# Loading half of one chunk by sixteen small transfers in a DMA-bound softmax

## The chip, the cores and the metric

The kernel runs on one core of a Trainium2 chip. The metric is device time in microseconds of one execution. The sixteen DMA engines move a transfer in packets, one row of a chunk each (32,000 packets of 32 KB for 250 full transfers of 128 rows in the kernel before). Each engine reports on the transfer's semaphore when its share is done; this moment is a **landing**, and each transfer of the kernel before has sixteen.

## The reference

```python
batch, seq, vocab = 16, 256, 32768
logits: float32 [16, 256, 32768], temperature = 1.0
scaled = logits / temperature
scaled = scaled - scaled.max(axis=-1, keepdims=True)
exp_scaled = np.exp(scaled)
return exp_scaled / exp_scaled.sum(axis=-1, keepdims=True)
```

That is a softmax over 4096 rows: 537 MB are read and 537 MB are written.

## The kernel before

Each row is cut into two halves, so there are 8192 half rows of 16384 numbers. 128 half rows, one per SBUF partition, make a group; a group is two chunks of [128 x 8192] float32, 4 MB each. There are 64 groups and 128 chunks. A chunk lives in one of six slots: it is loaded, reduced to its maximum on VectorE, exponentiated in place on ScalarE, scaled in place by both, and stored from the same slot. All transfers are issued by SyncE.

```python
_CW = 8192; _BUFS = 6; _LAST_DMA = 4096

def load(i):
    g, c = divmod(i, C)
    xs = xpool.tile([P, CW], fp32, tag="x", name="xs")
    slots[i] = xs
    # the first and the last group are loaded in halves of 4096 columns
    for s, n in spans(CW, _LAST_DMA if g in (0, G - 1) else CW):
        nc.sync.dma_start(out=xs[:, s : s + n],
                          in_=x[g * P : (g + 1) * P, c * CW + s : c * CW + s + n])
...
# order: loads of chunks 0 to 5, store 0, then store i and load i + 5
order = [("L", i) for i in range(min(_BUFS, n_chunks))] + [("S", 0)]
for i in range(1, n_chunks):
    order.append(("S", i))
    if i + _BUFS - 1 < n_chunks:
        order.append(("L", i + _BUFS - 1))
```

(Wrappers that keep the program order are left out above.)

## Time and profile before

The time before is 2494.8 us (median of 4, 2492.84 to 2495.53).

| what | value |
|---|---|
| DMA engines, share of slices at 90% or more | all but the last |
| rate over the span, over 1000 to 2000 us | 431 GB/s, 433 GB/s |
| packets of 32 KB (one row of a chunk): usual time | 1.213 us |
| packets of 16 KB: usual time | 0.611 us |
| landings of the last transfer, first and last of 16 engines | 2482.4 and 2492.9 us |

The page of the kernel before, busy shares and the first rows of its 40 time slices (a digit 9 is 90% or more):

```profile
span 2493.8 us, 2234 instructions
DVE 1487.4 (60%) x964; ACT 1405.0 (56%) x455; POOL 0.2 (0%) x4
...
DMA  9999999999999999999999999999999999999998
GB/s 412 433 430 432 429 431 432 433 433 434 433 434 432 435 432 435 432 435 431 436 431 435 432 434 433 434 433 433 433 433 433 433 433 434 434 433 434 432 431 368
```

VectorE and ScalarE have 40% to spare; the DMA engines have nothing. All slices but the first and the last lie at 429 to 436 GB/s. So the whole game is played for the last half per cent, the 431 GB/s over the span against the 433 GB/s from 1000 to 2000 us.

In this text the **shortfall** of a stretch is its length minus the bytes moved in it divided by 433.3 GB/s (sixteen packets of 32 KB every 1.21 us), with each packet's bytes spread evenly over its time; it is worked out from the packet records. Before, it is 3.6 us up to 80 us (mostly the start) and 2.0 us from 80 to 460 us. **Stretching** is the sum, over all packets, of the time above 1.213 or 0.611 us, where it exceeds 0.05 us. Nearly all of it falls before 460 us, in bursts 19.4 us apart, where the engines go over from a load to a store all at once: up to 230 us each burst starts in the last 1 to 3 us before a load lands (from 108 us on for the load that lands at 110.2 us). The worst burst comes earlier, from 58 us on, before the load that lands at 61.7 us; from 60 to 61 us the rate is 285 GB/s.

What SyncE waits for before it issues a transfer, in the kernel before (total, times, longest):

```profile
SPq L64 <- DMA out_dram<-xs: 2246.9, 122, 19.6
SPq L75 <- DVE xs L160: 73.4, 4, 39.7
SPq L224 <- DMA out_dram<-xs: 30.7, 3, 21.1
```

L64 is the load, L75 the store. Loads wait for the store that frees their slot; no load waits for another load.

The beginning of the chain of waits of the kernel before, from 8 us on (start, length, what):

```profile
2.68 29.61 DMA xs<-in_logits_dram
...
48.26 7.21 ACT xs L163 x2
...
55.48 26.44 DMA out_dram<-xs
...
82.38 38.48 DMA out_dram<-xs
...
121.31 38.66 DMA out_dram<-xs
```

The stores 0 and 1 are issued at 51.9 and 55.5 us, when they are computed, while the queues still hold loads up to about 62 us. From 82 us on the chain runs store by store in steps of about 39 us, four transfers each.

### The profile page before, as it was taken

To read this page: it belongs to the slowest core of one execution; us is meant where nothing else is said; L and a number is where in the kernel's file an instruction comes from. 1 tells how busy PE (TensorE), PEld (TensorE's weight loads), DVE (VectorE), ACT (ScalarE), POOL (GpSimd) and SP (SyncE) were. 2 spreads that over 40 slices of the span, in tenths; PEclk is the share of its full clock that TensorE was granted. 3 is DMA by queue.
4 is the path that set the end of the run, shared out by engine and by line. 5 is a ranking of instruction groups with operands and counts; after the bars stand their busy time and mean duration, and the time that the engine had idled before them with its cause. 6 is when DMAs were issued, how large, how long until landed. Compare 5 with 4: busy or idle time off the path is not lost.

```text
span 2493.8 us, 2234 instructions
## 1 busy us (share of the span) xinstructions
DVE 1487.4 (60%) x964; ACT 1405.0 (56%) x455; POOL 0.2 (0%) x4
## 2 busy tenths in 40 slices
DVE  7655565556655566555665566655666566655663
ACT  5665554655556555565555655555546555465553
POOL 0000000000000000000000000000000000000000
DMA  9999999999999999999999999999999999999998
GB/s 412 433 430 432 429 431 432 433 433 434 433 434 432 435 432 435 432 435 431 436 431 435 432 434 433 434 433 433 433 433 433 433 433 434 434 433 434 432 431 368
DMA packets 37745, 1073.90 MB, mean 431 GB/s; under 512 B 4192, under 2 KB 4192, under 8 KB 4192
## 3 DMA queue, kind: packets, MB, share of 16 engines
q1 hardware_dynamic: 37728, 1073.76, 99.9%
q14 instruction: 17, 0.14, 0.0%
HBM read 536.87 MB, written 536.87 MB: 431 GB/s over the span
## 4 chain that ended last, share of the span: by engine, by line
DMA 96%; SPq 1%; ACT 1%; DVE 1%; issue 1%; ACTq 0%
DMA out_dram<-xs 93%; DMA xs<-in_logits_dram 2%; SPq L64 1%; DVE nm L107 1%; ACT xs L163 1%; ACT xs L114 0%; ACTq L224 0%; SPq L75 0%; DVE f L150 0%; ACT ee L131 0%; DVE rS L149 0%; DVE Sh L87 0%; DVE ttj L138 0%; DVE Sh L84 0%; DVE Sh L138 0%
## 5 line engine op out<-in xcount | busy, mean ns | idle before, releaser
L114 ACT ACTIVATE xs<-xs,nm 128x8192 f32<-128x8192 f32 (+1 forms) x130 | 912.1, 7016 | 972.4 <-DVE nm L107 972.4
L107 DVE TENSOR_REDUCE nm<-xs 128x1 f32<-128x8192 f32 (+1 forms) x130 | 1111.6, 8551 | 527.3 <-DMA xs<-in_logits_dram 527.3
L163 ACT ACTIVATE xs<-xs,f 128x4096 f32<-128x4096 f32 (+1 forms) x130 | 468.1, 3648 | 71.4 <-DVE f L150 71.4
L160 DVE TENSOR_SCALAR xs<-xs,f 128x4096 f32<-128x4096 f32 (+1 forms) x130 | 295.7, 2318 | 3.7 <-DVE f L150 1.8
L138 DVE CUSTOM_DVE_ANT_0 ttj<-ee,ssum 128x2 f32<-128x2 f32 x64 | 10.3, 161 | 423.8 <-ACT ee L131 423.8
L114 ACT ACTIVATION_READ_ACCUMULATOR xs<-xs,nm 128x1 f32 x130 | 24.2, 186 | 0.0
L131 ACT ACTIVATE ee<-nm,nMh 128x2 f32<-128x2 f32 x64 | 17.9, 280 | 0.0
L150 DVE TENSOR_SCALAR f<-ee,rS 128x2 f32<-128x2 f32 x64 | 14.6, 229 | 2.2
L149 DVE RECIPROCAL rS<-Sh 128x1 f32<-128x1 f32 x64 | 10.5, 164 | 2.2
L87 DVE TENSOR_TENSOR nMh<-nMh 128x1 f32<-128x1 f32 x64 | 10.2, 160 | 2.2
L87 DVE TENSOR_TENSOR Sh<-Sh 128x1 f32<-128x1 f32 x64 | 10.2, 160 | 2.2
L129 DVE TENSOR_REDUCE nMh<-nm 128x1 f32<-128x2 f32 x64 | 9.9, 155 | 2.2
L84 DVE STREAM_SHUFFLE nMh<-nMh 128x1 f32<-128x1 f32 x64 | 9.7, 151 | 0.0
L84 DVE STREAM_SHUFFLE Sh<-Sh 128x1 f32<-128x1 f32 x64 | 9.7, 151 | 0.0
L114 ACT ACT_TABLE_LOAD x1 | 1.3, 1283 | 12.9 <-DMA xs<-in_logits_dram 12.9
L138 DVE DVE_READ_ACCUMULATOR2_ANT Sh<- 128x1 f32 x64 | 5.3, 84 | 0.0
L84 DVE LOAD_MASK_SELECT Sh<-Sh x64 | 0.9, 14 | 2.8
L84 DVE LOAD_MASK_SELECT nMh<-nMh x64 | 0.9, 14 | 2.7
L210 POOL MEMSET const-bfloat16-1.0<- 128x1 bf16 x1 | 0.1, 102 | 0.0
L210 POOL MEMSET const-uint8-127<- 128x1 uint8 x1 | 0.1, 102 | 0.0
L210 POOL MEMSET const-float32-0.0<- 128x1 f32 x1 | 0.1, 99 | 0.2 <-issue 0.2
L210 POOL MEMSET const-float32-1.0<- 128x1 f32 x1 | 0.1, 99 | 0.0
## 6 DMA issues: line engine op xcount, KB each, us to landing
out_dram<-xs SPq DMA_DIRECT2D x126, 4096.0 KB, 38.2
xs<-in_logits_dram SPq DMA_DIRECT2D x124, 4096.0 KB, 29.0
xs<-in_logits_dram SPq DMA_DIRECT2D x8, 2048.0 KB, 22.3
out_dram<-xs SPq DMA_DIRECT2D x4, 2048.0 KB, 26.7
```

Source lines behind the costliest of these rows:

```text
L64: nc.sync.dma_start(out=xs[:, s : s + n], in_=x[g * P : (g + 1) * P, c * CW + s : c * CW + s + n],)
L84: nc.vector.stream_shuffle(out=v[:, j + 1 : j + 2], in_=v[:, j : j + 1], mask=mask)
L87: nc.vector.tensor_tensor(out=v[:, j + 1 : j + 2], in0=v[:, j : j + 1], in1=v[:, j + 1 : j + 2], op=op,)
L107: nc.vector.tensor_reduce(out=nm[:, k : k + 1], in_=xs[:, s : s + n], axis=X, op=A.max, negate=True)
L114: nc.scalar.activation(out=xs[:, s : s + n], in_=xs[:, s : s + n], func=Exp, bias=nm[:, k : k + 1], scale=inv_t, accum_out=ssum[:, k : k + 1],
L129: nc.vector.tensor_reduce(out=nMh[:, 0:1], in_=nm, axis=X, op=A.min)
L131: nc.scalar.activation(out=ee, in_=nm, func=Exp, bias=nMh[:, n_rounds : n_rounds + 1], scale=-1.0,)
L138: nc.vector.tensor_tensor_reduce(out=ttj, in0=ee, in1=ssum, scale=1.0, scalar=0.0, op0=A.mult, op1=A.add, accum_out=Sh[:, 0:1],)
L149: nc.vector.reciprocal(out=rS, in_=Sh[:, n_rounds : n_rounds + 1])
L150: nc.vector.tensor_scalar_mul(out=f, in0=ee, scalar1=rS)
L160: nc.vector.tensor_scalar_mul(out=xs[:, s : s + cut], in0=xs[:, s : s + cut], scalar1=f[:, k : k + 1])
L163: nc.scalar.activation(out=xs[:, s + cut : s + n], in_=xs[:, s + cut : s + n], func=Copy, scale=f[:, k : k + 1],)
```

## The change: its intent and the diff

The sixteen DMA engines start in step: all sixteen landings of a transfer lie within 0.4 us up to 52 us. While in step they all change over from loads to stores at once. The change wants to set them apart at the start, by giving them unequal work once. The means are transfers of 15, 14, ... 1 and 8 rows of 16 KB.

```diff
+_LADDER = _BUFS - 1
...
-        for s, n in spans(CW, _LAST_DMA if g in (0, G - 1) else CW):
-            tc.keep_in_program_order(
-                nc.sync.dma_start(
-                    out=xs[:, s : s + n],
-                    in_=x[g * P : (g + 1) * P, c * CW + s : c * CW + s + n],
+        for s, n in spans(CW, _LAST_DMA if g in (0, G - 1) or i == _LADDER else CW):
+            steps = [P] if i != _LADDER or s else [*range(15, 0, -1), 8]
+            p = 0
+            for m in steps:
+                tc.keep_in_program_order(
+                    nc.sync.dma_start(
+                        out=xs[p : p + m, s : s + n],
+                        in_=x[g * P + p : g * P + p + m, c * CW + s : c * CW + s + n],
+                    )
                 )
-            )
+                p += m
+            assert p == P
```

Below, "ladder" is the series of sixteen transfers, and "second half" the ordinary transfer of the other 4096 columns of chunk 5 that follows it.

## The prediction

> **What bounds the kernel now.** The sixteen DMA engines. The page's engine rows give VectorE 60%, ScalarE 56%, DMA 90% or more in every slice and 431 GB/s. The chain of waits is 93.5% stores. The packet records leave almost nothing to gain: nearly all 32,000 packets of 32 KB take 1.213 us (half-size ones 0.611 us); packets of one engine start 1.21 us apart, plus 0.01 us per transfer for the semaphore write. 256 full transfers of 9.68 us plus the start at 1.8 us give 2482 us. [...]
>
> The span is 2493.8 us because one engine is late. Landings of the last transfer: eight engines within 0.5 us of 2482.4 us, others 3 to 7 us later, the last 10.5 us later. That spread was 0.35 us until 52 us, 4.9 at 343, 6.5 at 460, then grew about 0.7 per 310 us. Two causes: (a) until 460 us packets stretch to 1.3 to 2.4 us at the switches between loads and stores, every 19.4 us, while engines are in step, some 3 us per engine; (b) instruction fetches of 8 KB cost one engine about 0.7 us each[...].
>
> **What the change does.** Sixteen transfers of m rows of 16 KB. [...] It aims at (a), worth at most 5 us on the last engine. [...]
>
> **It will not be evenly spaced.** There are eight completion semaphores, and the timeline shows SyncE waiting, ahead of a transfer, for the transfer eight before it on the same semaphore. Before, this cost nothing. Now steps 14 to 11 wait for the half loads of chunks 0 and 1 (8 to 23 us), 10, 9, 8 for chunks 2, 3, 4 (32, 42, 52 us), later ones for earlier steps. So the second half, on all engines, is issued near 57 us and starts near 58 us. [...] The first store goes out near 57.5 us instead of 51.9 us. [...]stretching falls by perhaps half; fetches stay. Lateness of the last engine: 1.6 to 4.9 (delay) + 5 (fetches) + 0 to 4 (stretching), around 9.5 us instead of 10.5. VectorE and ScalarE have slack (chunk 5 lands at 62 us, is read at 70 us).
>
> **Predicted: 2494.0 us, range 2489.5 to 2498.0.** Chances: faster by over 2% 0.005, within 2% 0.99, slower by over 2% 0.005.
>
> **Right or wrong shows in:** the timeline at 52 to 58 us (SyncE's waits between small issues, GB/s dipping); fewer stretched packets between 60 and 460 us; the spread of the last landings; the first store landing near 76 us.
>
> **What would make it wrong:** small transfers not waiting (full stagger, perhaps 2490 us); [...]ten engines in step spreading as before on top of the delay.

The sum came to 1.6 to 4.9 us (delay) + 5 us (fetches) + 0 to 4 us (stretching), taken as around 9.5 us after 2482.4 us, against 10.5 us before. The delay was the author's estimate, from an assumed share of rows for each engine. For the fetches the trace before shows seven steps of 0.75 to 0.78 us, 5.3 us together.

## More of the kernel before

The 25 executions of the kernel before go from 2492.47 to 2501.62 us (0.4%), the four of its first round from 2492.84 to 2495.53 us; all profiled runs compared here had a granted clock (the share of full clock speed that the chip allowed) of 1.0.

Rates in five stretches of the kernel before. The columns are the stretch, its length, busy time of VectorE, ScalarE and GpSimd with numbers of instructions, clock, DMA share and GB/s:

```profile
16.00:50.00 34.00, 32.23 (x17) 23.57 (x8) 0.00 (x0) 1.00 1.02 439
50.00:80.00 30.00, 28.70 (x20) 28.36 (x10) 0.00 (x0) 1.00 1.00 421
80.00:100.00 20.00, 13.70 (x10) 13.40 (x5) 0.00 (x0) 1.00 0.98 421
100.00:460.00 360.00, 209.52 (x136) 200.67 (x64) 0.00 (x0) 1.00 1.00 431
460.00:2440.00 1980.00, 1185.48 (x767) 1122.27 (x361) 0.00 (x0) 1.00 1.00 433
```

A packet's bytes are put where it starts, so short stretches are rough. What is to be seen is that 433 GB/s is reached from 460 us on, and that between 50 and 460 us a little is missing.

## The result

The time is 2510.11 us (median of 4, 2509.46 to 2510.58) against 2494.8 us: 15.3 us longer, above the range. The ratio of the fast runs is 1.0062, with a 95% interval of 1.0045 to 1.0080. (A ratio here is the mean time of one kernel's fast runs over that of the other's of the same rounds, so not quite the ratio of the medians.) So it is slower beyond doubt, and still within 2%.

The page after, in the same lines:

```profile
span 2507.7 us, 2257 instructions
DVE 1487.6 (59%) x964; ACT 1405.1 (56%) x455; POOL 0.2 (0%) x4
...
DMA  9999999999999999999999999999999999999998
GB/s 357 374 432 432 432 433 434 433 433 433 433 434 434 433 431 434 433 434 432 432 434 433 435 432 431 434 433 435 433 431 434 433 434 433 432 433 433 434 430 378
```

Only the first two slices differ much, 357 and 374 GB/s instead of 412 and 433. Each is 62 us long. The digits of the DMA share say little here: a packet counts as busy for as long as it takes, and packets took longer (1.72 instead of 0.611 us, below). The same stretches after:

```profile
16.00:50.00 34.00, 32.22 (x17) 23.49 (x8) 0.00 (x0) 1.00 1.02 439
50.00:80.00 30.00, 19.72 (x15) 27.24 (x9) 0.00 (x0) 1.00 0.78 172
80.00:100.00 20.00, 10.78 (x13) 8.10 (x4) 0.00 (x0) 1.00 1.02 441
100.00:460.00 360.00, 210.55 (x136) 198.64 (x64) 0.00 (x0) 1.00 1.00 432
460.00:2440.00 1980.00, 1186.18 (x767) 1119.21 (x358) 0.00 (x0) 1.00 1.00 433
```

Everything happens between 50 and 80 us: 172 GB/s at a DMA share of 0.78. The shortfall of that stretch goes from 0.9 to 17.7 us (+16.7), and from 80 to 460 us it falls from 2.0 to 0.6 us (-1.4). Together that is +15.3 us. The two profiled executions differ by 13.9 us (2493.8 and 2507.7 us): another 1.4 us were won after 2440 us, where the last landings lie closer together. (That the two stretches give the difference of the medians, 15.3 us, to the digit is chance.) SyncE's waits after:

```profile
SPq L68 <- DMA out_dram<-xs: 2244.0, 122, 19.3
SPq L68 <- DMA xs<-in_logits_dram: 60.5, 17, 10.6
SPq L81 <- DVE xs L166: 33.7, 3, 24.7
```

L68 is now the load. The second line is new: loads wait for loads, 17 times. The timeline of SyncE between 40 and 80 us in the kernel after shows how long the ladder takes to issue (start, length, number of transfers merged):

```profile
42.11 25.91 SPq L68 DMA_DIRECT2D xs<-in_logits_dram  x11
68.91 2.37 SPq L81 DMA_DIRECT2D out_dram<-xs  x2
```

The first line ends with the issue of the second half at 67.7 us; the first store goes out at 68.9 us instead of 51.9. The instruction records of SyncE have each transfer with the semaphore it waits for and the one it raises (the time in us):

```
 4.18  15 rows  raises 108          53.00   8 rows  waits 107, raises 107
 8.00  14 rows  waits  99, raises  99    54.70   7 rows  waits 108, raises 108
12.88  13 rows  waits 100, raises 100    56.67   6 rows  waits  99, raises  99
17.77  12 rows  waits 101, raises 101    58.37   5 rows  waits 100, raises 100
22.67  11 rows  waits 103, raises 103    60.20   4 rows  waits 101, raises 101
32.40  10 rows  waits 105, raises 105    61.85   3 rows  waits 103, raises 103
42.11   9 rows  waits 106, raises 106    ...
                                         67.66 128 rows  waits 108, raises 108
```

There are eight semaphores, and each transfer waits for the one eight places before it. So far this is as predicted. But from 53 us on the steps follow each other every 1.2 to 2.0 us instead of every 0.6 us, because a row takes that long: the 16 KB packets that start between 50.9 and 58 us take 1.72 us in the mean, instead of 0.611 us. The chain of waits after, from 8 us on, has three links of loads where before it had one load and the computation:

```profile
12.88 45.47 DMA xs<-in_logits_dram
...
58.37 12.49 DMA xs<-in_logits_dram
...
70.93 30.33 DMA out_dram<-xs
...
101.73 38.25 DMA out_dram<-xs
```

The intent did come true in part. Stretching after 100 us fell from 31 to 10 us, and the last transfer's landings now spread over 8.3 us instead of 10.5 us. Not all of this can be put down to the ladder: a run without it that only loads chunk 5 in halves (e6_halves below) has a stretching of 19 us, and there is one trace of each, so a good part of the drop may be scatter. But all engines are late: the first landing of the last transfer is at 2498.5 instead of 2482.4 us.

### The profile page after: what moved, and what is told of

The parts are those of the page before. It is cut to its first block, busy times and chain, and to the rows that moved or that the text cites. A ratio compares the mean times of both kernels' runs of the same rounds, so it can differ in the third digit from the quotient of the medians.

```text
span 2507.7 us, 2257 instructions
## 1 busy us (share of the span) xinstructions
DVE 1487.6 (59%) x964; ACT 1405.1 (56%) x455; POOL 0.2 (0%) x4
## 4 chain that ended last, share of the span: by engine, by line
DMA 97%; SPq 1%; ACT 0%; issue 0%; DVE 0%; ACTq 0%
DMA out_dram<-xs 93%; DMA xs<-in_logits_dram 4%; SPq L68 1%; ACT xs L169 0%; DVE nm L113 0%; ACT xs L120 0%; ACTq L230 0%; SPq L81 0%; DVE f L156 0%; ACT ee L137 0%; DVE rS L155 0%; DVE Sh L93 0%; DVE ttj L144 0%; DVE Sh L90 0%; DVE Sh L144 0%
## 5 line engine op out<-in xcount | busy, mean ns | idle before, releaser
L155 DVE RECIPROCAL rS<-Sh 128x1 f32<-128x1 f32 x64 | 10.5, 164 | 2.2
```

The costliest lines, as they stand in the source:

```text
L155: nc.vector.reciprocal(out=rS, in_=Sh[:, n_rounds : n_rounds + 1])
```

## The experiments

**The theories.** P: the rows of a small transfer lie in neighbouring SBUF partitions and slow each other there. What asks for an explanation is the 113 GB/s between 52 and 60 us of the change, with 10 to 15 packets in work at a time. Rival H: the neighbouring rows of the input collide in HBM. Rival W: the small transfers are slow by themselves, or the late waits on the eight semaphores are what costs. The strides of nine and eight below were chosen by an assumption on which partitions belong together. No trace shows it; the runs show what each stride costs.

A table first. "To 80 us" is the shortfall up to 80 us, "stretching" that after 100 us. The difference is between medians of the same rounds.

| run | ladder | time, us | difference | to 80 us | stretching |
|---|---|---|---|---|---|
| before | none | 2494.8 | | 3.6 | 31 |
| after | stride 1 | 2510.11 | +15.3 | 20.4 | 10 |
| e1_both9 | stride 9 | 2499.30 | +4.6 | 8.4 | 19 |
| e2_sbuf9 | stride 9 in SBUF only | 2499.20 | +4.5 | 8.0 | 19 |
| e3_hbm9 | stride 9 in the input only | 2510.07 | +15.4 | 20.8 | 12 |
| e5_both8 | stride 8 | 2503.33 | +8.8 | 14.4 | 10 |
| e6_halves | none, chunk 5 in halves | 2494.50 | 0.0 | 3.6 | 19 |
| e7_inter1 | stride 1, issued early | 2510.99 | +16.5 | 20.4 | 17 |
| e4_inter9 | stride 9, issued early | 2500.70 | +6.0 | 9.9 | 5 |
| e8_own | eight steps from partition 0 | 2494.26 | -0.2 | 3.9 | 6 |
| e9_foreign | eight steps from partition 64 | 2497.49 | +3.0 | 7.3 | 5 |
| e10_own8k | as e8, rows of 8 KB | 2493.15 | -1.4 | 3.9 | 7 |

The runs e2, e3, e5, e6 and e7 were timed once, so their state is unknown (their clock is 1.0); what is read from them are packet times and shortfalls first. The diffs below are shortened and simplified to what each run changes.

### Rows spread over the partitions: e1_both9

The rows of each transfer lie nine partitions apart instead of one. The sixteen transfers keep their numbers of rows and order, and cover all partitions.

```diff
+_STEPS = [(0, 15), (2, 14), (3, 13), (4, 12), (5, 11), (6, 10), (7, 9), (1, 8), (73, 7), (80, 6), (88, 5), (96, 4), (104, 3), (112, 2), (120, 1), (8, 8)]
...
-                        out=xs[p : p + m, s : s + n],
-                        in_=x[g * P + p : g * P + p + m, c * CW + s : c * CW + s + n],
+                        out=xs[a : a + 9 * (m - 1) + 1 : 9, s : s + n],
+                        in_=x[g * P + a : g * P + a + 9 * (m - 1) + 1 : 9, c * CW + s : c * CW + s + n],
```

> The change with the same sixteen transfers, but the rows of each taken with a stride of nine partitions (and nine rows of the input)[...]. Theory P[...]: small packets take about 0.61 us instead of 1.0 to 2.1, the second half is issued near 57 us instead of 67.7, the first store near 58 instead of 68.9, the shortfall between 50 and 80 us falls from 17.7 us to 3 to 5 us, and the time is 2493 to 2498 us. Rival W (each small transfer is slow by itself, or the waits on the eight semaphores alone cost the time): packets and issue times stay as in the change, 2508 us or more. Rival H (neighbouring rows of the input collide in HBM): as P in this run; the next two tell.

Measured: 2499.30 us, against 2494.71 us before in the same rounds (ratio 1.0015, 0.9999 to 1.0030). The small packets take 0.65 us. The timeline of SyncE between 40 and 80 us of this run:

```profile
42.08 16.85 SPq L72 DMA_DIRECT2D xs<-in_logits_dram  x11
59.18 0.82 SPq L85 DMA_DIRECT2D out_dram<-xs  x2
```

The same eleven issues take 16.85 instead of 25.91 us; the second half goes out at 58.5 us, the first store at 59.2 us. The waits on the semaphores are still there (this run's load-for-load waits):

```profile
SPq L72 <- DMA xs<-in_logits_dram: 42.5, 7, 9.5
```

About 11 of the 15 us are gone; what is left in the time is not clear of the noise (the runs before on this chip go from 2492.77 to 2501.62 us), but the shortfall shows it. Since the number of transfers, their order and the waiting rule are untouched, this speaks for P or H. The shortfall between 50 and 80 us was expected at 3 to 5 us and is 5.7 us; that rest is taken up below.

### SBUF or HBM: e2_sbuf9 and e3_hbm9

Both give wrong results, as rows of one tile are permuted.

```diff
 e2_sbuf9
-                        in_=x[g * P + a : g * P + a + 9 * (m - 1) + 1 : 9, ...],
+                        in_=x[g * P + p : g * P + p + m, ...],
 e3_hbm9
-                        out=xs[a : a + 9 * (m - 1) + 1 : 9, ...],
+                        out=xs[p : p + m, ...],
```

> Only the SBUF side of the ladder is strided by nine; the rows of the input are read as neighbours, as in the change. The result is wrong on purpose (rows of one tile permuted). Theory P: as the run with both sides strided (small packets 0.61 us, second half issued near 57 us, about 2495 us). Rival H: as the change (packets 1.6 to 2 us, second half near 68 us, about 2508 us or more).

> Only the input side of the ladder is strided by nine; SBUF partitions are neighbours, as in the change. The result is wrong on purpose. Theory P: as the change (packets 1.6 to 2 us, second half issued near 68 us, about 2508 to 2511 us). Rival H: fast as the run with both sides strided, about 2495 us.

Measured: 2499.20 us with only the SBUF side spread, 2510.07 us with only the input side spread. The timelines of SyncE between 40 and 80 us, first e2_sbuf9:

```profile
42.09 16.48 SPq L72 DMA_DIRECT2D xs<-in_logits_dram  x11
58.70 0.82 SPq L85 DMA_DIRECT2D out_dram<-xs  x2
```

and e3_hbm9:

```profile
42.23 26.94 SPq L72 DMA_DIRECT2D xs<-in_logits_dram  x11
70.21 2.19 SPq L85 DMA_DIRECT2D out_dram<-xs  x2
```

The small packets take 0.63 and 1.79 us. The side that matters is SBUF. Rival H is out.

### A dose in between: e5_both8

The rows of each transfer lie eight partitions apart instead of one or nine.

```diff
+_STEPS = [(0, 15), (1, 14), ..., (7, 8), (70, 7), ..., (120, 1), (71, 8)]   # stride 8
```

> The change with a stride of eight partitions instead of one or nine[...]. Theory P: in between. [...]small packets 0.9 to 1.3 us in the stage near 55 us, second half issued near 62 us (58.5 with stride nine, 67.7 with stride one), shortfall between 50 and 80 us 8 to 13 us, time 2500 to 2506 us. If only the nearness of partitions counted[...] it would be as stride nine, 2499 us.

Measured: 2503.33 us; small packets 1.16 us; second half issued at 62.8 us; shortfall between 50 and 80 us 11.6 us. All are in the expected ranges. With strides of 1, 8 and 9 partitions the packets take 1.72, 1.16 and 0.65 us. So it is not the nearness of the partitions alone, or eight and nine would hardly differ; which partitions are in each other's way is not shown.

### The split alone: e6_halves

```diff
-            steps = [P] if i != _LADDER or s else [*range(15, 0, -1), 8]
+            steps = [P]
```

> The ladder alone undone: chunk 5 is loaded by two transfers of half width, both over all 128 partitions. Theory P and its rivals alike: as the kernel before (2492 to 2497 us), shortfall between 50 and 80 us about 1 us. If splitting the chunk cost something by itself, it shows here.

Measured: 2494.50 us, as before (2494.47 in the same rounds). Loading chunk 5 in halves costs nothing that shows in this one run.

### Engines never idle: e4_inter9 and e7_inter1

The ladder is issued in fours behind the loads of chunks 1, 2, 3 and 4. The intent was that the transfer eight places before is long done when it is waited for, and that the queues never run dry. Only the second came true, as the waits below show. e4_inter9 has stride nine, e7_inter1 stride one.

```diff
             load(i)
             loaded = i + 1
+            if 1 <= i < _LADDER:
+                ladder(4 * i - 4, 4 * i)     # four of the sixteen small transfers
```

> Strided by nine on both sides, and the sixteen small transfers issued in fours behind the loads of chunks 1, 2, 3 and 4, so that none of the waits on the eight semaphores comes late. Theory: the DMA engines never idle; shortfall between 50 and 80 us under 1.5 us; the first store is issued near 52 us as before; [...]stretching after 100 us under 10 us in sum instead of 31 us before. [...]the last landing is 10 to 14 us after the first and the first at about 2477.6 us; time 2489 to 2496 us, within 0.2% of the kernel before. If the idea behind the change held in full (even spacing makes all engines faster), it would be clearly faster than before, by more than 5 us.

> The small transfers over neighbouring partitions, as in the change, but issued in fours behind the loads of chunks 1 to 4, so that no wait on the eight semaphores comes late. Theory P: [...]the DMA engines are all in use, [...]the shortfall up to 80 us (9.9 us in the same order with stride nine, 3.6 us before) is over 15 us in all and the time 2505 to 2515 us. Rival W (the late waits are what costs): about as the same order with stride nine, 2499 to 2502 us.

Measured: e7_inter1 2510.99 us, as bad as the change itself. SyncE's waits for loads and the rates of e7_inter1:

```profile
SPq L89 <- DMA xs<-in_logits_dram: 46.8, 12, 10.1
SPq L73 <- DMA xs<-in_logits_dram: 18.0, 5, 9.0
...
16.00:50.00 34.00, 24.72 (x16) 21.92 (x7) 0.00 (x0) 1.00 1.02 285
50.00:80.00 30.00, 17.23 (x15) 17.65 (x6) 0.00 (x0) 1.00 0.99 346
```

L89 is the ladder, L73 the other loads. So the waits were not taken away: there are 17 of them as in the change (64.8 us in all against 60.5), and the first store goes out at 66.1 us (55.2 in e4_inter9), not near 52 us. What the order did take away is idle engines: from 16 to 80 us at least 15 packets are in work at any time, where in the change the number falls to 5 near 67 us. The time stays as bad. With the waits kept and the rows spread (e1_both9), two thirds of the loss went away. So neither the waits nor the idle engines alone make the 15 us, and rival W is out as their source; that they add something is not excluded. No run removes the waits themselves.

e4_inter9 is a miss: 2500.70 us instead of 2489 to 2496. Its stretching is nearly gone (5 us after 100 us), but the shortfall up to 80 us is 9.9 us, not the start's 2.7 us plus at most 1.5 us. Its packets of 16 KB and 32 KB slow down in three stages, around 25, 38 and 52 us, with 235, 231 and 207 GB/s in the worst microsecond, and each is where small rows run beside full transfers. No store is issued before 55.2 us.

### From partition 0 or from partition 64: e8_own and e9_foreign

A new theory, F: what is left of the cost with stride nine comes from small rows beside full transfers, and it depends on which partitions they are written to. So eight extra transfers of 8 to 1 rows, four partitions apart, start at partition 0 in one run and at partition 64 in the other, with all else equal. (The labels "own" and "foreign" come from an assumption of the author's on which engine writes which partitions in a full transfer. No trace shows it, as the packet records have neither engine numbers nor partitions, and what the expectations said of it is cut, with the 4.9 us that e8_own's gave for the most loaded engine.) The extra transfers load part of chunk 5's data early; chunk 5's own transfer loads everything again, so the result is right.

```diff
+    def extra(ks):
+        for k in ks:
+            m = 8 - k
+            a = _BASE + k % 4 + 32 * (k // 4)     # _BASE = 0 (e8_own), 64 (e9_foreign)
+            e = a + 4 * (m - 1) + 1
+            nc.sync.dma_start(out=xs[a:e:4, 0:4096],
+                              in_=x[g * P + a : g * P + e : 4, c * CW : c * CW + 4096])
...
+            if i == 2: extra(range(0, 4))         # behind the load of chunk 2
+            elif i == 3: extra(range(4, 8))
```

> The kernel before, with eight extra transfers of 8 down to 1 rows of 16 KB behind the loads of chunks 2 and 3 (the data are loaded once more by chunk 5's own transfer; the result is right). Rows four partitions apart from partition 0[...]. Theory F[...]: no dip in GB/s between 20 and 55 us, packets 0.61 us, and the time is before's plus 0 to 4 us: 36 extra rows are 1.4 us per engine in the mean[...], against less stretching; 2489 to 2498 us. If any small transfer or any break of the lockstep dips the throughput, it dips here as well.

> As the run before it, but the rows start at partition 64[...]; counts, sizes, strides and times of issue are the same. Theory F: throughput dips where the extra rows meet full transfers (stretched packets between 20 and 50 us over 30 us in sum against under 10 in the run before), and the time is 2 to 6 us longer than in the run before. Without such collisions: no difference.

Measured: 2494.26 us (ratio 0.9998, 0.9983 to 1.0012) and 2497.49 us (1.0011, 0.9994 to 1.0028). Neither is clear of the kernel before, but the two differ from each other: 2494.07 to 2494.32 against 2497.37 to 2497.71 us. The rates while the extra rows run and after, e8_own:

```profile
20.00:52.00 32.00, 30.22 (x17) 25.49 (x9) 0.00 (x0) 1.00 1.01 436
52.00:80.00 28.00, 20.68 (x16) 20.98 (x7) 0.00 (x0) 1.00 1.00 415
```

and e9_foreign:

```profile
20.00:52.00 32.00, 29.86 (x17) 25.27 (x8) 0.00 (x0) 1.00 1.02 378
52.00:80.00 28.00, 20.81 (x16) 20.98 (x8) 0.00 (x0) 1.00 1.00 432
```

436 against 378 GB/s, with the same bytes, sizes and order of issue (the times of issue agree within 0.1 us up to 22.7 us; after that e9_foreign falls behind, as its transfers land later). Stretching up to 50 us is 8 us from partition 0 and 81 us from partition 64. In the second lines e8_own pays once for its changeover to stores (415 GB/s, packets around 60 us stretched) and e9_foreign does not (432 GB/s); why is not shown. From partition 0 the small transfers cost nothing that shows; from partition 64 the same transfers do cost. The full packets lose too, not only the small ones: at 48.5 us only two small rows are in work in e9_foreign, and all fourteen full packets beside them take 2.15 to 2.55 us instead of 1.213; why they slow down stays open. At the worst, from 34 to 36 us, the whole core moves 213 GB/s. The change's second half, which starts at 68.7 us beside the last small rows and runs at 129 to 194 GB/s until 75 us, shows the same pattern, and most of what e1_both9 has left may come from it as well. The landings fit: the last small row lands at 77.3 us in the change and at 64.0 us in e1_both9, and from there on both move at least 422 GB/s. For these two it is argued from the same pattern, not shown by a run of its own.

### Trying for a version that beats both: e10_own8k, e11_actstore, e12_own8k_act

e10_own8k halves the rows of e8_own (`4096` columns to `2048`), and with them the extra bytes.

> The own-partition ladder with rows of 8 KB instead of 16: half the extra bytes[...]. [...] If the stretching stays low (under 25 us in sum from 50 us on), the last landing comes 1 to 3 us earlier than with 16 KB: 2491 to 2494 us; if the half stagger no longer keeps the engines apart, as before, 2494 to 2496 us.

Measured: 2493.15 us (2493.01 to 2493.23) against 2494.57 us before (2493.59 to 2495.49). It went in the expected direction, and no run of it is as slow as the fastest one before of the same rounds, but the ratio is 0.9994 with an interval of 0.9977 to 1.0010. It is not shown to be faster.

e11_actstore issues the stores of the kernel before from ScalarE. It was meant to test whether instruction fetches, which the prediction blamed for about 5 us, make the last engine late. The author took them for SyncE's, which issues half as many transfers in this run.

```diff
 def store(i):
-                nc.sync.dma_start(
+                nc.scalar.dma_start(
```

> The kernel before with its stores issued by ScalarE instead of SyncE. Theory of the instruction fetches[...]: [...]the lateness of the last engine falls from 10.5 to 7 or 8 us, 2491 to 2494 us. If the fetches are not what makes the last engine late, no change, or slower where ScalarE waits at its stores.

> Both together: the 8 KB own-partition ladder and the stores from ScalarE. If both effects are real and add: 2488 to 2492 us, the only version under both kernels by more than their scatter; if either is not, between 2491 and 2495 us.

Both failed as tests: 2926.75 us and 2921.04 us, 17% slower. The page of e11_actstore, its busy shares, GB/s and its two queues:

```profile
DVE 1481.6 (51%) x964; ACT 1405.2 (48%) x455; POOL 0.2 (0%) x4
...
DMA  9988989889898888988889898898988989888898
GB/s 415 388 348 360 379 354 384 347 359 380 358 380 347 363 372 359 378 353 373 358 358 380 351 387 349 360 379 354 382 349 359 380 359 379 346 366 373 359 380 380
...
q10 hardware_dynamic: 18720, 536.88, 44.4%
q1 hardware_dynamic: 19008, 536.88, 43.5%
```

With stores in a queue of their own, VectorE waits 1380 us for loads instead of 527 us, and the DMA engines run idle 12% of the time. Why is not shown. Whether the fetches make the last engine late is not shown by a run. The trace before speaks for it: a fetch is a packet of 8 KB that takes 0.31 us, and the spread of a transfer's landings grows by 0.75 to 0.78 us at each of seven fetches 311 us apart (447 to 2310 us), 5.3 us together, and not at the other fetches after 760 us. Whose fetches these seven are the records do not say; from one of them to the next SyncE starts 64 instructions and VectorE 128.

## Why the prediction was wrong, point by point

- **What bounds the kernel: right.** DMA engines at 433 GB/s before and after; the compute engines never entered the result.
- **The eight semaphores: right in mechanism.** The steps wait as described, and the new line of load-for-load waits (60.5 us) is there. But keeping the engines supplied while the rows stay neighbours gained nothing (e7_inter1, 2510.99 us).
- **"The second half, on all engines, is issued near 57 us": the step that failed.** It rested on 0.611 us for a row of 16 KB, a duration read from full transfers. In the ladder a row takes 1.72 us in the mean, because the rows of a step lie in neighbouring partitions (0.65 us with stride nine). The second half went out at 67.7 us, and the first store landed at 91.6 instead of 76 us. With the rows spread (e1_both9) the same program issues it at 58.5 us, so the rest of the sum was nearly right. (The time of e1_both9, 2499.30 us, is still above the predicted range: the next point has the second reason.) The error was to carry a duration over from full transfers to small ones: the trace before has no transfer of fewer than 128 rows, so it could not show what these cost.
- **"1.6 to 4.9 (delay)": wrong in size,** for the same reason, and perhaps for a second one: small rows beside full transfers can slow the full packets as well (2.15 to 2.55 instead of 1.213 us in e9_foreign, 378 GB/s against 436 in e8_own). The first landing of the last transfer came 16.0 us later, and the lateness of the last engine, put at about 9.5 us after 2482.4 us, was 24.3 us.
- **That most engines would start the second half together and some a few us later: about right in shape.** After the ladder the first store's landings have eleven engines within half a microsecond and the last about 3.8 us behind; at the end ten engines are within 0.5 us.
- **"Stretching falls by perhaps half": right in direction, too small.** From 31 to 10 us after 100 us. With the ladder issued early at stride nine (e4_inter9) it is 5 us. But 26 us of stretching are 1.6 us of time on each of sixteen engines. This is what the change could win at the most beyond the late engine, and 1.4 us were won up to 460 us; e6_halves, without the ladder, already has 0.7 us of them in its one trace.
- **"Fetches stay" (5 us on the last engine):** not tested, as e11_actstore failed; the steps of 0.75 to 0.78 us in the trace before, 5.3 us in seven fetches, agree with it.

So the kernel lost 16.7 us in thirty microseconds and got 1.4 us back over the next 380.

## What to carry to other kernels

When a transfer is cut into pieces of a few partitions, ask which partitions each piece writes, and time a packet of such a piece instead of taking the duration from a full transfer: here a stride of nine instead of one took 11 of 15 us away. Small transfers beside full ones cost nothing that showed when they started at partition 0 (436 GB/s), and 3 us when the same ones started at partition 64 (378 GB/s). And before engines are set apart to avoid their collisions, work out the prize: 31 us of stretched packets over sixteen engines were 2 us of 2495.
